# Where the weight tiles and the split x tiles begin in SBUF: 64 more bytes in two tiles

## The chip, the cores and the metric

The kernel runs on one core of a Trainium2 chip. The metric is the device time of one execution in microseconds (us), as the median of several executions. A profile is a record of one execution.

## What is computed

One decoder block on a sequence of 2048 tokens with 1024 channels, batch 1. The input is normalised (RMSNorm), scaled and shifted by a conditioning vector, and projected by one wide matrix. From that projection two branches are fed, a gated causal convolution and an RWKV-7 recurrence; each is projected again, the two are mixed by sigmoid gates, and an output projection is added to the input through a gate.

```python
h = _rmsnorm(x, norm_g[l]) * (1.0 + scale[:, None, :]) + shift[:, None, :]
p = jnp.einsum('bsd,de->bse', h, w_in[l])
c_val, c_gate, c_og, ts, r_og, g_conv, g_rwkv = jnp.split(p, SPLITS, axis=-1)
y_conv = _conv_branch(c_val, c_gate, c_og, conv_k[l], ...)
y_rwkv = _rwkv7_branch(ts, r_og, rwkv_mu[l], ...)
m = jax.nn.sigmoid(g_conv) * y_conv + jax.nn.sigmoid(g_rwkv) * y_rwkv
out = jnp.einsum('bsd,de->bse', m, w_out[l])
x = x + gate[:, None, :] * out
...
return _rmsnorm(x, final_g)
```

## The kernel before

The sequence is worked in four blocks of 512 tokens (`TB`). Channels lie on the 128 partitions, eight tiles of 128 channels (`KT`).

The large projections keep float32 accuracy by splitting each operand into a high part rounded to the matmul's format and the remainder, and by three matmuls: high by high, high by low, low by high. `load_w` (from L176) gives a pair of weight tiles `w_hi` and `w_lo`, each 128 partitions by 4096 bytes; at first use it loads a raw tile `w_st`, rounds it (ScalarE, L189), subtracts (GpSimd or VectorE, L191) and stores both parts to DRAM; later uses load the two parts (L182, L183). All three are buffers of one tag in the pool `whl`, seven in a ring. `hsplit` (from L358) makes `h_hi` and `h_lo`, the split x tiles, eight of each, 2048 bytes a partition, in the pool `hp`.

`mm3k` (L199 to L206) is the inner loop. The weight tile is the stationary operand and is loaded into the array for each matmul; the split x tile streams past it. In the first phase (`msplit` 2) a block's 512 columns are streamed in two matmuls of 256; this is the group `ps_main<-h_hi,w_hi` and its two sisters at L206. In the second phase (`msplit` 1) the two branch projections stream 512 columns (`o_hi`, `u_hi`, `m_hi` against `w_hi` and `w_lo`, L206 too), and the output projection (L1090 to L1092) has the operands the other way round: the mixed tiles `m_hi`, `m_lo` or `o_hi`, `o_lo` stationary, the weight tiles streaming 256 columns.

Between the projections the order on TensorE is that of the tile scheduler. In each group of two channel tiles (`pair`, called from `group`) the recurrence adds small matmuls (L534, L597, L657, L666, L684, L689, L695, L708) and a chain of GpSimd steps (L625, L627); the convolution (`conv`) is 31 VectorE steps per channel tile (L774).

SBUF is given out in two stacks, every tile rounded up to 32 bytes a partition. The left one begins with 1152 bytes of scratch and constants, then the pool `cst` (identity, the vectors, small columns, `hlg` and `hlb`), then `whl`, then `c1`, `l3`, `lt`. The right one grows down from the top: `e1` (the pair's tiles), `xp`, `hp`, `e2`. `cst` holds 1856 bytes, which is 14.5 times 128, so that `whl` begins at byte 3008. In `e1` the tile `E1` has 2080 bytes, 16.25 times 128. Where tiles begin, as bytes past a multiple of 128:

| tiles | before | after |
|---|---|---|
| `w_hi`, `w_lo`, `w_st` (3008 + 4096 n before) | 64 | 0 |
| `h_hi`, `h_lo` (159680 + 2048 n before) | 64 | 0 |
| the `xp` ring (`xt`, `hf`, `z` ...), `lw`, `la`, `wl`, `M`, `ta` | 64 | 0 |
| `th` and `t1` (one tag in `e2`), `yj` | 0 | 64 |
| `KR`, `As`, `uv`, `tk`, `BK`, `S`, `XO`, `La`, `TT` | 96 | 32 |
| `E2`, `k`, `sq`, `r`, `rh` (after `E1` in `e1`) | 96 | 96 |
| `o_hi`, `o_lo`, `mr`, `xt0` to `xt7` (second phase, right) | 32 | 32 |
| `m_hi`, `m_lo`, `u_hi`, `u_lo` (second phase, left) | 32 | 96 |
| `w_f`, the weight tiles of two of the first projections | 96 | 32 |

Of the kernel before, what the change touches and what calls it, by code (L numbers as in the profile page):

```python
# [9 lines left out]
F32 = mybir.dt.float32  # L10
# [8 lines left out]
P = 128  # L19
D = 1024  # L20
KT = D // P
TB = 512
NTT = TB // P
CH = 64
NCH = TB // CH
# [56 lines left out]
def hybrid_block(ctx: ExitStack, tc: tile.TileContext, x, vecs, convk, w2a2, final_g, ada, w_in, w_co, w_ro, w_o, crow, out,  # L82
# [6 lines left out]
    cst = ctx.enter_context(tc.tile_pool(name="cst", bufs=1))  # L89
# [22 lines left out]
    def vc(name, j=None):  # L112
        o, w = VOFF[name]
        return v[:, o:o + w] if j is None else v[:, o + j:o + j + 1]
# [140 lines left out]
    e1 = early.enter_context(tc.tile_pool(name="e1", bufs=1, side="right"))  # L255
# [9 lines left out]
    nc.sync.dma_start(v, vecs)  # L265
    ab = vc("ada_b")
    hlg = cst.tile([P, KT], F32, name="hlg")
    hlb = cst.tile([P, KT], F32, name="hlb")
    nc.vector.tensor_scalar(out=hlg, in0=vc("conv_ln_g"), scalar1=0.5, scalar2=None, op0=ALU.mult)
    nc.vector.tensor_scalar(out=hlb, in0=vc("conv_ln_b"), scalar1=0.5, scalar2=None, op0=ALU.mult)  # L270

# [167 lines left out]
    def ch3(ap):  # L439
        return ap.rearrange("p (c t) -> p c t", t=CH)  # L440
# [15 lines left out]
    def pair(b, q_, pr, h, lora, uv, Asb, rn, res):  # L456
# [18 lines left out]
        for half in range(2):  # L475
            cs = slice(half * TB // 2, (half + 1) * TB // 2)
            nc.vector.tensor_tensor_scan(out=M[:, cs], data0=keepm, data1=M[:, cs], initial=0.0, op0=ALU.mult, op1=ALU.add)
        E1 = e1.tile([P, NCH, CH + 1], F32, name="E1", tag="E1", bufs=1)
        nc.gpsimd.memset(E1[:, :, 0:1], 1.0)
        nc.scalar.activation(E1[:, :, 1:], ch3(M), AF.Exp, scale=-DECAY)  # L480
        E2 = e1.tile([P, TB], F32, name="E2", tag="E2")
        nc.scalar.activation(E2, M, AF.Exp, scale=DECAY)
        pe = l3.tile([P, NCH], F32, name="pe", tag="pe", bufs=4)
        nc.gpsimd.tensor_copy(pe, E1[:, :, CH])

# [6 lines left out]
        k4 = k.rearrange("p (c e t) -> p c e t", e=2, t=CH)  # L492
        E1x = E1[:, :, 0:CH].rearrange("p (c e) t -> p c e t", e=2)
        E1i = E1[:, :, 1:].rearrange("p (c e) t -> p c e t", e=2)
        E24 = E2.rearrange("p (c e t) -> p c e t", e=2, t=CH)
# [77 lines left out]
    def group(b, g, h, lora, fill):  # L573
        uv = l3.tile([P, NCH, 2, P], F32, name="uv", tag="uv", bufs=2)
        As = [l3.tile([P, 2, NCH, P], F32, name="As", tag="As", bufs=ASB) for _ in range(2)]
        R = [{}, {}]
        rn = lt.tile([P, 2, NCH // 2, 2], F32, name="rn", tag="rn")
        pairs = [pair(b, q, 2 * g + q, h, lora, uv, As[q], rn, R[q]) for q in range(2)]
        for i, q in enumerate(ORD):
            next(pairs[q])  # L580
# [589 lines left out]
```

## Time and profile before

| what | value |
|---|---|
| median of 3 runs | 3031.91 us (3030.95 to 3034.19) |
| the profiled execution's own time | 3047.45 us |
| its span, first to last instruction | 3045.7 us |
| mean granted TensorE clock | 0.975 |
| busy share of the span | TensorE 96%, weight loads 90%, VectorE 68%, GpSimd 41%, ScalarE 31% |
| DMA traffic | 699.24 MB in 368673 packets, mean 230 GB/s |

PE is TensorE's matmuls, PEld its weight loads, DVE VectorE, ACT ScalarE, POOL GpSimd, SP the queue that issues the DMAs. Matmuls overlap in the records, so that the busy time of one is longer than the distance to the next; where it says so, the text takes the distance between the starts in the timeline. In a group's row the numbers are the count, the busy time, the mean duration of one, and the engine's idle time just before them with what ended it.

### The profile page before, as it was taken

The page shows a single profiled execution, that of the slowest core. Times are in us where ns is not written, and L with a number is a line of the kernel's source. Part 1 is how long each engine was busy: PE and PEld are TensorE (multiplying, and loading weights), DVE is VectorE, ACT ScalarE, POOL GpSimd, SP SyncE. Part 2 cuts the span into 40 slices and gives each one's busy share as a digit, 9 for nine tenths or more (in the row PEclk, how much of TensorE's full clock was granted, in tenths as well). Part 3 has the DMA queues.
Part 4 walks back from the last instruction along what each step waited for, and adds up shares of the span by engine and source line. Part 5 has one row for each costly group of instructions (what it writes and reads, how often), then busy time and mean ns, then how long its engine had stood idle before and what let it go on. Part 6 is the DMA issues. An engine that isn't in the chain of part 4 may idle for free.

```text
span 3045.7 us, 64763 instructions
## 1 busy us (share of the span) xinstructions
PE 2914.9 (96%) x25672; PEld 2735.9 (90%) x25672; DVE 2058.4 (68%) x3896; ACT 935.2 (31%) x1759; POOL 1250.1 (41%) x1786
## 2 busy tenths in 40 slices
PE   6999998999999999899999999999999999899998
PEld 6889998989989899899999999999999988788988
DVE  6587877686867676668676767676779635776433
ACT  4433434332323232233232323232323222333201
POOL 3455555434343425143434263625467204565000
PEclk9899999999999999999999999999999999999999
DMA  8666758564758578847474777655647778889674
GB/s 303 205 234 209 251 196 282 199 235 145 250 185 260 187 242 287 235 137 246 151 246 139 246 254 252 199 185 165 212 141 246 229 264 309 320 311 344 239 280 163
DMA packets 368673, 699.24 MB, mean 230 GB/s; under 512 B 136241, under 2 KB 154993, under 8 KB 368370
## 3 DMA queue, kind: packets, MB, share of 16 engines
q1 hardware_dynamic: 368370, 695.10, 68.0%
q8 instruction: 202, 3.31, 0.4%
q14 instruction: 101, 0.83, 0.1%
HBM read 506.14 MB, written 187.70 MB: 228 GB/s over the span
## 4 chain that ended last, share of the span: by engine, by line
PE 61%; DMA 16%; DVE 9%; POOL 7%; SPq 3%; issue 2%; ACT 2%; ACTq 0%; DVEq 0%; POOLq 0%
PE ps_main L206 43%; DMA w_st<-w_in_t 3%; PE aux L534 2%; POOL TT L627 2%; POOL itmp L625 2%; DMA w_st<-w_ro_t 2%; DMA w_st<-w_co_t 2%; PE pout L1091 2%; PE pout L1092 2%; PE pout L1090 2%; PE xo L689 2%; DVE acc L774 1%; DMA w_gr<-grow_d 1%; PE xo L684 1%; PE xo L695 1%
## 5 line engine op out<-in xcount | busy, mean ns | idle before, releaser
L206 PE MATMUL ps_main<-h_hi,w_hi 128*128 128x256 f32 x4608 | 971.3, 289 | 12.2 <-ACT w_hi L189 3.4
L206 PE MATMUL ps_main<-h_hi,w_lo 128*128 128x256 f32 x4608 | 965.4, 289 | 8.5 <-POOL w_lo L191 5.0
L206 PE MATMUL ps_main<-h_lo,w_hi 128*128 128x256 f32 x4608 | 971.3, 289 | 0.0
L206 PEld LDWEIGHTS ps_main<-h_hi,w_hi 128*128 128x128 f32 x4608 | 735.3, 194 | 24.1 <-ACT w_hi L189 3.9
L206 PEld LDWEIGHTS ps_main<-h_hi,w_lo 128*128 128x128 f32 x4608 | 731.8, 194 | 17.5 <-POOL w_lo L191 6.3
L206 PEld LDWEIGHTS ps_main<-h_lo,w_hi 128*128 128x128 f32 x4608 | 733.9, 194 | 8.1 <-issue 0.5
L774 DVE SCALAR_TENSOR_TENSOR acc<-u,ck,acc 128x512 f32<-128x512 f32 x928 | 698.6, 753 | 20.8
L625 POOL TENSOR_TENSOR itmp<-La,TT 128x126 f32<-128x126 f32 (+22 forms) x496 | 180.2, 363 | 140.9 <-DMA La<-dA 106.1
L627 POOL TENSOR_TENSOR TT<-TT,itmp 128x126 f32<-128x126 f32 (+22 forms) x496 | 188.2, 379 | 37.3
L681 ACT ACTIVATE Se<-S,pe 128x128 f32<-128x128 f32 x256 | 89.0, 395 | 239.4 <-DVE S L699 239.2
L191 POOL TENSOR_TENSOR w_lo<-w_st,w_hi 128x1024 fp32r<-128x1024 f32 x47 | 113.6, 2417 | 112.8 <-ACT w_hi L189 106.2
L699 DVE TENSOR_TENSOR S<-xo,Se 64x128 f32<-64x128 f32 x256 | 73.5, 287 | 104.1 <-PE xo L695 100.8
L189 ACT CAST w_hi<-w_st 128x1024 fp32r<-128x1024 f32 x71 | 74.2, 1046 | 182.4 <-DMA w_st<-w_in_t 147.4
L534 PE MATMUL aux<-KR,BK 64*128 64x128 f32 x1024 | 121.5, 307 | 7.4 <-POOL BK L517 4.1
L534 PEld LDWEIGHTS aux<-KR,BK 64*128 64x128 f32 x1024 | 104.2, 208 | 18.7 <-POOL BK L517 4.3
L562 POOL TENSOR_TENSOR BK<-BK,pe 128x1024 f32<-128x1024 f32 x32 | 62.0, 1939 | 140.7 <-PE aux L534 113.1
L691 DVE TENSOR_TENSOR uv<-xo,rn 64x256 f32<-64x256 f32 x128 | 53.8, 420 | 90.7 <-PE xo L689 88.8
L686 DVE TENSOR_TENSOR XO<-xo,XO 128x256 f32<-128x256 f32 x128 | 53.7, 420 | 89.9 <-PE xo L684 70.5
L537 DVE TENSOR_TENSOR As<-aux,maskA 128x512 f32<-128x512 f32 x128 | 83.8, 685 | 36.9 <-PE aux L534 35.6
L684 PE MATMUL xo<-S,KR 128*128 128x128 f32 x512 | 83.0, 285 | 15.0 <-DVE S L699 14.9
L786 ACT ACTIVATE th<-ps_main 128x512 f32<-128x512 f32 x64 | 38.1, 596 | 190.1 <-PE ps_main L206 168.9
L431 ACT ACTIVATE t<-ps_main,mu 128x512 f32<-128x512 f32 x96 | 65.6, 683 | 97.4 <-PE ps_main L206 90.4
(301 smaller groups left out, 5318.2 us busy)
## 6 DMA issues: line engine op xcount, KB each, us to landing
w_hi<-kh_in SPq DMA_DIRECT2D x219, 512.0 KB, 5.1
w_lo<-kl_in SPq DMA_DIRECT2D x219, 512.0 KB, 4.0
w_st<-w_in_t SPq DMA_DIRECT2D x73, 512.0 KB, 4.9
kh_in<-w_hi SPq DMA_DIRECT2D x71, 512.0 KB, 2.9
kl_in<-w_lo SPq DMA_DIRECT2D x71, 512.0 KB, 3.7
w_hi<-kh_ro SPq DMA_DIRECT2D x32, 512.0 KB, 5.6
w_lo<-kl_ro SPq DMA_DIRECT2D x32, 512.0 KB, 5.5
w_hi<-kh_co SPq DMA_DIRECT2D x32, 512.0 KB, 5.5
```

The lines of the kernel that those rows point to most:

```text
L189: nc.scalar.copy(hi, st)
L191: lo_eng.tensor_tensor(out=lo, in0=st, in1=hi.bitcast(F32), op=ALU.subtract)
L206: nc.tensor.matmul(ps[:, qs], ww[:, k, :], aa[k][:, qs], start=(k == 0 and t == 0 and q == 0), stop=(k == KT - 1 and t == 2 and q == ms - ...
L431: nc.scalar.activation(t1, ps, AF.Identity, scale=mu1[:, mi:mi + 1])
L534: nc.tensor.matmul(pA[hh][:, c // 2, es], BK[hs, cc, es], KR[hs, cc, es], start=(c == 0), stop=(c == 3), skip_group_check=True)
L537: nc.vector.tensor_tensor(out=Asb[:, hh, c4 * 4:c4 * 4 + 4, :].rearrange("p (a e) n -> p a (e n)", e=2), in0=pA[hh], in1=flat(maskA).unsqu ...
L625: nc.gpsimd.tensor_tensor(out=tmp[:, :ni, :nt], in0=La[:, j:j + 1, j + 1:].broadcast_to([P, ni, nt]), in1=TT[:, :ni, j:j + 1].broadcast_to ...
L627: nc.gpsimd.tensor_tensor(out=TT[:, :ni, j + 1:], in0=TT[:, :ni, j + 1:], in1=tmp[:, :ni, :nt], op=ALU.add)
L681: nc.scalar.mul(Se[:, q, :], Sg[:, q, :], R[q]["pe"][:, c:c + 1])
L684: nc.tensor.matmul(xo[:, q, :], R[q]["KR"][:, cc, es], Sg[:, q, :], start=(q == 0), stop=(q == 1), skip_group_check=True)
L699: nc.vector.tensor_tensor(out=Sg[hs, :, hs], in0=xo[hs, 2:4, hs], in1=Se[hs, :, hs], op=ALU.add)
L774: nc.vector.scalar_tensor_tensor(out=acc if i + 1 < HALO else yj, in0=u[:, i:i + TB], scalar=ck[:, j, i:i + 1], in1=acc, op0=ALU.mult, op1 ...
```

## The change

Two tiles get 64 more bytes a partition. `hlb` is taken as the first eight columns of a tile of 24, which moves everything above it on the left stack up by 64 bytes. `E1` gets 67 instead of 65 columns for each of its eight chunks, all at the end; it is taken flat and its first 520 columns are viewed as before, which moves `E1` and everything below it on the right stack down by 64 bytes. No instruction, no shape and no order in the program text is changed.

```diff
-    hlb = cst.tile([P, KT], F32, name="hlb")
+    hlb = cst.tile([P, 24], F32, name="hlb")[:, :KT]
...
-        E1 = e1.tile([P, NCH, CH + 1], F32, name="E1", tag="E1", bufs=1)
+        E1 = e1.tile([P, NCH * (CH + 3)], F32, name="E1", tag="E1", bufs=1)
+        E1 = E1[:, :NCH * (CH + 1)].rearrange("p (c t) -> p c t", c=NCH)
         nc.gpsimd.memset(E1[:, :, 0:1], 1.0)
         nc.scalar.activation(E1[:, :, 1:], ch3(M), AF.Exp, scale=-DECAY)
```

## Prediction, made before the changed kernel ran

> **What bounds the kernel now.** I read the page first: its shares, the chain, the costliest groups.
>
> ```profile
> span 3045.7 us, 64763 instructions
> PE 2914.9 (96%) x25672; PEld 2735.9 (90%) x25672; DVE 2058.4 (68%) x3896; ACT 935.2 (31%) x1759; POOL 1250.1 (41%) x1786
> ...
> PE ps_main L206 43%; DMA w_st<-w_in_t 3%; PE aux L534 2%; POOL TT L627 2%; POOL itmp L625 2%; DMA w_st<-w_ro_t 2%; DMA w_st<-w_co_t 2%; PE pout L1091 2%; PE pout L1092 2%; PE pout L1090 2%; PE xo L689 2%; DVE acc L774 1%; DMA w_gr<-grow_d 1%; PE xo L684 1%; PE xo L695 1%
> ...
> L206 PE MATMUL ps_main<-h_hi,w_hi 128*128 128x256 f32 x4608 | 971.3, 289 | 12.2 <-ACT w_hi L189 3.4
> L206 PE MATMUL ps_main<-h_hi,w_lo 128*128 128x256 f32 x4608 | 965.4, 289 | 8.5 <-POOL w_lo L191 5.0
> L206 PE MATMUL ps_main<-h_lo,w_hi 128*128 128x256 f32 x4608 | 971.3, 289 | 0.0
> ```
>
> TensorE works almost all the time, and 43% of the chain is one line, the matmuls of the split x tiles with the weight tiles: 3 x 4608 = 13824 of 256 columns. Both their operands are the tiles that the change moves. The view of busy time by stretch puts TensorE at 2313 of 2392 us in the first phase (then weight loads, VectorE, ScalarE, GpSimd, the granted clock, the DMA share and GB/s); the view of its waits shows how little it loses to transfers.
>
> ```profile
> 60.00:2452.00 2392.00, 2313.22 (x22197) 2215.94 (x22195) 1707.98 (x3139) 761.50 (x1400) 1064.97 (x1646) 0.97 0.66 215
> ```
> ```profile
> PE ps_main L206 <- DMA w_lo<-kl_in: 3.5, 3, 2.5
> ...
> PE pout L1091 <- DMA w_lo<-kl_o: 2.0, 1, 2.0
> ```
>
> So the question is the distance between matmul starts, and whether it depends on where the tiles begin. The timeline of TensorE gives it, in undisturbed stretches at the full clock: first phase, front stage (weights `w_f`), output projection with `o` tiles and with `m` tiles, branch projection of 512 columns.
>
> ```profile
> 1501.46 0.40 PE L206 MATMUL ps_main<-h_hi,w_lo 128*128 128x256 f32 x2
> ...
> 1504.34 0.40 PE L206 MATMUL ps_main<-h_hi,w_lo 128*128 128x256 f32 x2
> ```
> ```profile
> 56.25 0.64 PE L206 MATMUL ps_f<-h_hi,w_f 128*128 128x256 f32 x4
> ...
> 57.45 0.40 PE L206 MATMUL ps_f<-h_lo,w_f 128*128 128x256 f32 x2
> ```
> ```profile
> 2855.35 0.28 PE L1090 MATMUL pout<-w_hi,o_hi 128*128 128x256 f32 x1
> ...
> 2857.80 0.28 PE L1090 MATMUL pout<-w_hi,o_hi 128*128 128x256 f32 x1
> ```
> ```profile
> 2718.86 0.28 PE L1090 MATMUL pout<-w_hi,m_hi 128*128 128x256 f32 x1
> ...
> 2721.35 0.28 PE L1090 MATMUL pout<-w_hi,m_hi 128*128 128x256 f32 x1
> ```
> ```profile
> 2841.00 0.39 PE L206 MATMUL ps_main<-u_hi,w_hi 128*128 128x512 f32 x1
> ...
> 2845.90 0.39 PE L206 MATMUL ps_main<-u_hi,w_hi 128*128 128x512 f32 x1
> ```
>
> First phase: 12 rows of two, 24 matmuls in 2.88 us, 120.0 ns each. Front: 10 in 1.20 us, 120 ns. Output projection with `o`: 21 in 2.45 us, 116.7 ns; with `m`: 21 in 2.49 us, 118.6 ns. 512 columns: 21 in 4.90 us, 233.3 ns, which is 116.7 for each 256.
>
> **What these distances say of alignment.** By the table of addresses: in the first phase weight and x tile both begin 64 past a multiple of 128, and the distance is 120. In the front the weight begins 96 past, x 64 past: 120 again. In the output projection the streaming weight begins 64 past, the stationary tile 32 past: 116.7 with `o`, 118.6 with `m`. At 512 columns the streaming tile is 32 past: no more per column than the best. So streaming from 64 past a multiple of 128 does not by itself cost 120, and the weight's move from 64 to 96 changed nothing. On the other side `o` and `m` differ by 1.9 ns with the same shapes and the same remainder, so something besides shape, perhaps the addresses' relation, is worth up to 3.3 ns. None of these has both operands on a multiple of 128: that case no row shows.
>
> **The change part by part.** No instruction is added or removed, and no wait; `E1` keeps its two disjoint writes, so I expect the same order on every engine. Four effects are left.
>
> *First-phase matmuls.* Bounds from the rows: from 116.7, the best distance for 256 columns, to 123.3, as far above 120 as that is below (no row is there; it is the observed spread turned over). That is 13824 x 3.3 ns = 46 us either way on TensorE. What of it reaches the end: all of it if TensorE stays the bound (97% busy in the phase), or the share of these matmuls that lies on the chain. The chain has 43% of 3045.7, 1310 us; all matmuls of L206 take 13824 x 0.120 + 1344 x 0.233 = 1972 us (1344 are those of 512 columns); 1310/1972 is 0.66, so 31 us. I take 0, because the two rows with equal structure and different weight alignment (first phase and front) agree at 120.
>
> *Second phase.* The `o` tiles stay, the weights move by 64; 1536 matmuls of the output projection, half with `o`: if these went from 116.7 to 120, 768 x 3.3 ns = 2.5 us more; if the `m` half went from 118.6 to 116.7, 768 x 1.9 ns = 1.5 us less. I take 0.
>
> *VectorE and ScalarE.* The convolution's steps read `u` at starts 4 bytes apart, so every remainder is already in this row; and ScalarE writes from PSUM into `th` (0 past) and `rk` (96 past):
>
> ```profile
> L774 DVE SCALAR_TENSOR_TENSOR acc<-u,ck,acc x928: 704/756/1139, 151.0 to 2407.6; 128x512 f32<-128x512 f32 x186
> ```
> ```profile
> L754 ACT ACTIVATE th<-ps_main 128x512 f32<-128x512 f32 x64 | 38.0, 594 | 160.4 <-PE ps_main L206 108.3 <-issue 43.2 <-DMA gr_d<-th 3.7
> ...
> L557 ACT COPY rk<-aux 128x512 f32<-128x512 f32 x32 | 18.8, 586 | 1.5 <-PE aux L287 0.8
> ```
>
> Minimum and median are 7% apart over all starts, and 586 to 594 ns over remainders 0 and 96: no cost to move, none to gain. `th` loses its alignment at no more than 8 ns. The cover is TensorE: VectorE is at 71% of the first phase.
>
> *DMA.* Stores from `th` and `yj` (0 past), `oc` and `vv` (96 past), and the weight traffic (64 past), to landing:
>
> ```profile
> ro_d<-th SPq DMA_DIRECT2D x32, 256.0 KB, 4.2
> bv_d<-vv SPq DMA_DIRECT2D x32, 256.0 KB, 2.3
> ...
> y_d<-yj SPq DMA_DIRECT2D x32, 256.0 KB, 3.6
> o_d<-oc SPq DMA_DIRECT2D x32, 256.0 KB, 4.6
> ```
> ```profile
> w_hi<-kh_in SPq DMA_DIRECT2D x219, 512.0 KB, 5.1
> ```
>
> The aligned stores (4.2 and 3.6) are not quicker than the others (2.3 and 4.6). If weight loads nevertheless became quicker, the two longest waits of TensorE for them come to 3.5 + 2.0 = 5.5 us, about the most it could give directly; slower by a tenth, 0.5 us each, they would still land within the ring of seven tiles. I take 0 from a range of -6 to +3.
>
> A rule that speaks for a gain here: the Trainium skill, "DMA: Bandwidth & Descriptors", section "How a descriptor splits into AXI transactions", says that transactions start on 256-byte boundaries, so that a run beginning off one needs one more. By it a 4096-byte row of a weight tile, now 192 past such a boundary and then on it, goes from 17 transactions to 16; by my estimate from the page that is up to 6% of these transfers, and the sum would still be within the 6 us above. The landing rows do not show such an order.
>
> **Sum.** 0 + 0 + 0 + 0. The profiled execution, 3047.45 us by itself (span 3045.7 and 1.75 around it), is 15.5 us over the median of the runs, 3031.91; with no term to subtract I give the median, a little rounded down for the DMA term: 3031 us. A measurement of this kernel can tell about 0.2%, 6 us, from no change.
>
> **The rivals.** *Same pace, same time* (my forecast): 3026 to 3038.
>
> *Alignment frees the matmuls.* The 120 would be a collision between the weight load and the streaming read, and the new addresses would end it, as `o` shows at 116.7. For it: `o` against `m`, equal but for the place. Against it: the front's 120. Price 31 us by the chain's share and 46 in full: 3001 to 2986; a half step to 118.6 gives 1.4/3.3 of 31, 13 us, 3019.
>
> *Alignment frees them altogether.* Then only the weight loads would set the distance. Matmuls of 128 columns with a load each show that floor:
>
> ```profile
> 1500.66 0.60 PE L695 MATMUL xo<-uv,tk 128*128 128x128 f32 x4
> 1500.99 0.28 PE L695 MATMUL xo<-uv,tk 128*128 128x128 f32 x1
> ```
>
> Three distances from the first start to the last matmul's start take 0.33 us, 110 ns. From 120 to 110 is 13824 x 10 ns = 138 us, 91 by the chain's share: 2941, down to 2894. Against it: the 512-column stretch, with its streaming tile at another remainder (32), does not beat 116.7 per 256 either. The Trainium skill, "TensorE: Matmul & The Clock Gate", section "Back-to-back issue gap", has 262 cycles for 256 columns, by my estimate 109 ns at its 2.4 GHz; it does not speak of alignment, and no full-clock stretch quoted here reaches it.
>
> *Slower: the same collision gets worse.* Place: L206 in the first phase. The distance between the two operands' starts changes by 128 bytes, as the weights go up by 64 and x goes down by 64. If the new relation costs what the good one saves, 123.3 ns, the kernel ends at 3031.9 + 31 to 46: 3062 to 3078. It decides from 120.7 ns on, where 13824 x 0.7 x 0.66 passes 6 us. For it: nothing but that relation has been seen to matter; against it: 120 is the longest steady distance in any stretch read here.
>
> **How the numbers follow.** Same pace 0.46. Freed to 116.7 or half of it 0.33. Freed altogether 0.04. Worse 0.11. A drift of some 10 us with unchanged distances, from throttling that falls otherwise (the clock's mean is 0.97 in the first phase), 0.06, half to each side for lack of a sign. Faster 0.33 + 0.04 + 0.03 = 0.40; within 0.2% 0.46; slower 0.14. The range takes in the freed case to its full price, 2986, and the drift and the small end of the worse one, to 3050; left out are the 0.04 below and most of the 0.11 above. The likeliest case alone has 3026 to 3038.
>
> **What would show it.** Right: the row of `ps_main<-h_hi,w_hi` keeps a mean of 289 ns, and 24 matmuls in an undisturbed stretch take 2.88 us; the landing times of weight tiles and the 756 of L774 stay. The freed case shows 2.80 us for 24 and less TensorE time with more waits on VectorE and GpSimd. The worse case shows over 2.90 us. The prediction fails if the distance depends on the relation of the two starts, which the rows here can't separate from the order of the matmuls.

## The result, and the profile after

The changed kernel takes 3023.47 us (median of 11 executions, 3016.2 to 3037.63), the kernel before 3034.06 us (median of 11): a ratio of 0.9965, 95% interval 0.9952 to 0.9979, or 10.6 us less. The profiled execution took 3030.42 us. From its page (span, busy times, the chain by engine, groups, a DMA row):

```profile
span 3028.7 us, 64763 instructions
PE 2896.6 (96%) x25672; PEld 2719.3 (90%) x25672; DVE 2058.4 (68%) x3896; ACT 935.8 (31%) x1759; POOL 1252.0 (41%) x1786
...
PE 56%; DMA 16%; DVE 10%; POOL 9%; issue 3%; SPq 3%; ACT 3%; ACTq 0%; DVEq 0%; POOLq 0%
...
L206 PE MATMUL ps_main<-h_hi,w_hi 128*128 128x256 f32 x4608 | 966.6, 288 | 12.2 <-DVE carry L437 3.6
...
L775 DVE SCALAR_TENSOR_TENSOR acc<-u,ck,acc 128x512 f32<-128x512 f32 x928 | 698.0, 752 | 20.8
...
w_hi<-kh_in SPq DMA_DIRECT2D x219, 512.0 KB, 5.2
```

Before, the chain by engine was this:

```profile
PE 61%; DMA 16%; DVE 9%; POOL 7%; SPq 3%; issue 2%; ACT 2%; ACTq 0%; DVEq 0%; POOLq 0%
```

The counts of instructions are those of before, and on each engine their order is too; line numbers from L477 on are one higher. VectorE's busy time is the same 2058.4, the convolution step 752 against 753 ns, a weight load lands after 5.2 against 5.1 us. What went down is TensorE's busy time, by 18.3 us. The mean of an L206 matmul fell by 1 ns only, but busy times overlap, and the distance between starts says more. TensorE's timeline of the changed kernel, first phase:

```profile
1501.06 0.40 PE L206 MATMUL ps_main<-h_hi,w_lo 128*128 128x256 f32 x2
...
1502.96 0.40 PE L206 MATMUL ps_main<-h_lo,w_hi 128*128 128x256 f32 x2
```

Eight rows of two lie between the two starts: 16 matmuls in 1.90 us, 118.75 ns, where it was 120.0. Over all undisturbed first-phase stretches (full granted clock, no wait in front of the matmul) the mean is 118.72 (119.74 before). The output projection with `o` tiles went the other way:

```profile
2855.08 0.28 PE L1091 MATMUL pout<-w_hi,o_hi 128*128 128x256 f32 x1
...
2857.60 0.28 PE L1091 MATMUL pout<-w_hi,o_hi 128*128 128x256 f32 x1
```

21 matmuls in 2.52 us, 120.0 ns; it was 116.7.

### The profile page after: what moved, and what is told of

Same layout as the page of the kernel before. It is cut to its first block, busy times and chain, and to the rows that moved or that the text cites. A ratio compares the mean times of both kernels' runs of the same rounds, so it can differ in the third digit from the quotient of the medians.

```text
span 3028.7 us, 64763 instructions
## 1 busy us (share of the span) xinstructions
PE 2896.6 (96%) x25672; PEld 2719.3 (90%) x25672; DVE 2058.4 (68%) x3896; ACT 935.8 (31%) x1759; POOL 1252.0 (41%) x1786
## 4 chain that ended last, share of the span: by engine, by line
PE 56%; DMA 16%; DVE 10%; POOL 9%; issue 3%; SPq 3%; ACT 3%; ACTq 0%; DVEq 0%; POOLq 0%
PE ps_main L206 41%; POOL TT L628 3%; POOL itmp L626 3%; DMA w_st<-w_in_t 2%; DMA w_st<-w_ro_t 2%; PE aux L535 2%; DMA w_st<-w_co_t 2%; PE pout L1092 2%; PE pout L1093 2%; PE pout L1091 2%; DMA w_gr<-grow_d 1%; PE xo L690 1%; DVE acc L775 1%; PE xo L696 1%; PE xo L685 1%
## 5 line engine op out<-in xcount | busy, mean ns | idle before, releaser
L206 PE MATMUL ps_main<-h_hi,w_hi 128*128 128x256 f32 x4608 | 966.6, 288 | 12.2 <-DVE carry L437 3.6
L206 PE MATMUL ps_main<-h_lo,w_hi 128*128 128x256 f32 x4608 | 967.1, 288 | 0.0
L206 PE MATMUL ps_main<-h_hi,w_lo 128*128 128x256 f32 x4608 | 960.7, 288 | 5.9 <-DMA w_lo<-kl_in 3.3
L206 PEld LDWEIGHTS ps_main<-h_hi,w_hi 128*128 128x128 f32 x4608 | 726.7, 191 | 24.1 <-DVE carry L437 3.9
L206 PEld LDWEIGHTS ps_main<-h_hi,w_lo 128*128 128x128 f32 x4608 | 723.4, 191 | 13.9 <-DMA w_lo<-kl_in 3.7
L206 PEld LDWEIGHTS ps_main<-h_lo,w_hi 128*128 128x128 f32 x4608 | 725.7, 191 | 8.1 <-issue 0.2
L191 POOL TENSOR_TENSOR w_lo<-w_st,w_hi 128x1024 fp32r<-128x1024 f32 x47 | 113.3, 2411 | 107.9 <-ACT w_hi L189 91.9
L535 PE MATMUL aux<-KR,BK 64*128 64x128 f32 x1024 | 114.9, 294 | 3.8 <-POOL TT L621 2.2
L535 PEld LDWEIGHTS aux<-KR,BK 64*128 64x128 f32 x1024 | 98.1, 196 | 14.5 <-POOL TT L621 2.4
L690 PE MATMUL xo<-XO,As 64*64 64x64 f32 x1024 | 90.6, 227 | 4.8 <-DVE XO L687 4.7
```

The lines of the kernel that those rows point to most:

```text
L191: lo_eng.tensor_tensor(out=lo, in0=st, in1=hi.bitcast(F32), op=ALU.subtract)
L206: nc.tensor.matmul(ps[:, qs], ww[:, k, :], aa[k][:, qs], start=(k == 0 and t == 0 and q == 0), stop=(k == KT - 1 and t == 2 and q == ms - ...
L535: nc.tensor.matmul(pA[hh][:, c // 2, es], BK[hs, cc, es], KR[hs, cc, es], start=(c == 0), stop=(c == 3), skip_group_check=True)
L690: nc.tensor.matmul(xo[pr_, q, hs], As[q][pr_, hh, c, kcol(e)], XO[pr_, c, q, hs], start=(q == 0 and hh == 0), stop=(q == 1 and hh == 1), s ...
```

## The experiments

Three theories went in. *Multiples of 128*: a tile that begins on a multiple of 128 bytes is read faster. *Order*: the distance hangs on the order of the three matmuls and on which half of the PSUM bank (the memory that takes the results) is written. *Relation*: what counts is d, the start of the streaming tile minus the start of the stationary one, modulo some power of two; the expected texts of the two halves take the same difference the other way round, so that their 64 is d = 192 here. In bytes modulo 256, weight and x tiles begin at 192 and 192 before (d = 0), and at 0 and 128 after (d = 128).

### Half of the change: the weight tiles alone

```diff
-    hlb = cst.tile([P, KT], F32, name="hlb")
+    hlb = cst.tile([P, 24], F32, name="hlb")[:, :KT]
```

> Only hlb's tile grows: weight tiles begin on a multiple of 128 (0 past a multiple of 512), split x tiles stay 64 past (448 past a multiple of 512). Relation theory (the distance of 256-column matmuls follows the difference of the two starts): the difference goes from 0 to 64, neither the 0 of before (120.0 ns) nor the 128 of after (118.7 ns); the first phase's distance differs from 120.0 and the time follows it by about 9 us per ns. Own-alignment theory (each operand by itself): the weight on a multiple of 128 gives its part alone, between 118.7 and 120.0 ns, 0 to 11 us faster. Rival, that the gain is not in the matmuls' distance: 120.0 ns and yet another time than before.

3013.51 us against 3036.65 of before, measured beside it: 0.9929 (0.9907 to 0.9950). One half of the change gains more than twice what the whole does. Now d is 192 - 0 = 192. Its timeline:

```profile
1819.90 0.39 PE L206 MATMUL ps_main<-h_lo,w_hi 128*128 128x256 f32 x2
...
1822.62 0.39 PE L206 MATMUL ps_main<-h_lo,w_hi 128*128 128x256 f32 x2
```

Twelve rows of two, 24 matmuls in 2.72 us: 113.3 ns, below anything seen before the change.

### The other half: the x tiles alone

```diff
-        E1 = e1.tile([P, NCH, CH + 1], F32, name="E1", tag="E1", bufs=1)
+        E1 = e1.tile([P, NCH * (CH + 3)], F32, name="E1", tag="E1", bufs=1)
+        E1 = E1[:, :NCH * (CH + 1)].rearrange("p (c t) -> p c t", c=NCH)
```

> Only E1 grows: split x tiles begin on a multiple of 128 (384 past a multiple of 512), weight tiles stay 64 past (448). Relation theory: the difference is 64 as with the weights alone, so the same first-phase distance and the same time as that kernel, to 0.2%. Own-alignment theory: the rest of the gain, so that the two kernels' gains add up to the 10.6 us of the whole change. In the output projection nothing moves but the relation stays: 116.7 ns with o tiles, about 118 with m tiles.

3019.27 us, 0.9941 (0.9919 to 0.9962). Two stretches of its timeline:

```profile
1819.79 0.39 PE L206 MATMUL ps_main<-h_lo,w_hi 128*128 128x256 f32 x2
...
1822.51 0.39 PE L206 MATMUL ps_main<-h_lo,w_hi 128*128 128x256 f32 x2
```
```profile
2069.98 0.40 PE L206 MATMUL ps_main<-h_hi,w_hi 128*128 128x256 f32 x2
...
2072.81 0.40 PE L206 MATMUL ps_main<-h_hi,w_hi 128*128 128x256 f32 x2
```

The first has 113.3 ns again (24 in 2.72 us), the second 117.9 (24 in 2.83). Both paces occur with the same d, each held through a stretch; the mean over all is 114.8. The two halves have different tiles on a multiple of 128 but the same d, 192, and the same pace, and their times are 5.8 us apart, within the 0.2% expected. Their gains, 23.1 and 17.4 us, don't add up to that of the whole. That speaks for the relation.

### The whole change once more

> The changed kernel once more beside its two halves: ratio 0.995 to 0.998 to before, first-phase distance 118.7 ns by every theory.

3029.06 us, 0.9980 (0.9965 to 0.9995), undisturbed mean 118.71 ns. On the same chip, against the same 3036.65 us of before, the whole gains 7.6 us, the weights alone 23.1 and x alone 17.4.

### A map of starts

All other work is left out here, and the one execution ran at the full granted clock. 16 stationary tiles and 16 streaming tiles begin at 0, 32, ... 480 modulo 512, `wa` to `wp` and `xa` to `xp`; each pair runs 48 matmuls into one half of a PSUM bank (L34), and once more into both halves in turn (L42).

```python
for w in ws:
    for t in xs:
        for i in range(48):
            nc.tensor.matmul(ps[:, 0:N], w, t[:, 0:N], start=(i == 0), stop=(i == 47))
```

> Matmuls alone: 16 weight tiles wa to wp that begin 0, 32 ... 480 bytes past a multiple of 512 against 16 streaming tiles xa to xp that do the same, 48 matmuls of 256 columns for each pair, first into one half of a bank (L39), then in turn into both halves as mm3k does (L47). All other work of the block is left out; the output is a copy of the input. Relation theory: the distance is constant along the diagonals of the table, 120.0 where the starts are equal, and both ways of writing give one table. Own-alignment theory: rows and columns with 0, 128, 256, 384 stand out. Order theory (the way the two halves of a bank are written sets 120 against 116.7): the first table is 116.7 throughout, the second 120. Carried over from the traces: w 448, x 448 gives 120.0; w 160, x 448 gives 116.7; w 0, x 384 gives 118.7; w 160, x 0 gives 120.0.

Rows of the timeline, 48 matmuls each (start, then the time of the 48). The stationary tile `wc` begins at 64, `wd` at 96:

```profile
228.67 6.02 PE L34 MATMUL pa<-xc,wc 128*128 128x256 f32 x48 [0.52 <-ACT sink L35]
235.21 5.87 PE L34 MATMUL pa<-xd,wc 128*128 128x256 f32 x48 [0.52 <-ACT sink L35]
241.59 5.92 PE L34 MATMUL pa<-xe,wc 128*128 128x256 f32 x48 [0.52 <-ACT sink L35]
248.03 6.02 PE L34 MATMUL pa<-xf,wc 128*128 128x256 f32 x48 [0.52 <-ACT sink L35]
254.56 5.96 PE L34 MATMUL pa<-xg,wc 128*128 128x256 f32 x48 [0.52 <-ACT sink L35]
261.04 5.97 PE L34 MATMUL pa<-xh,wc 128*128 128x256 f32 x48 [0.52 <-ACT sink L35]
267.52 5.72 PE L34 MATMUL pa<-xi,wc 128*128 128x256 f32 x48 [0.52 <-ACT sink L35]
273.76 5.95 PE L34 MATMUL pa<-xj,wc 128*128 128x256 f32 x48 [0.52 <-ACT sink L35]
280.23 6.02 PE L34 MATMUL pa<-xk,wc 128*128 128x256 f32 x48 [0.52 <-ACT sink L35]
...
338.22 6.02 PE L34 MATMUL pa<-xd,wd 128*128 128x256 f32 x48 [0.52 <-ACT sink L35]
...
377.07 5.73 PE L34 MATMUL pa<-xj,wd 128*128 128x256 f32 x48 [0.52 <-ACT sink L35]
```

From `xc` to `xj` d goes from 0 to 224 in steps of 32; at `xk`, d = 256, the time of d = 0 is back. `xd,wd` (d = 0) and `xj,wd` (d = 192), 32 bytes further up, repeat `xc,wc` and `xi,wc`. The row's time is 47 distances and the last matmul. The distance between starts, the first seven of each row left out, as the median over the 64 pairs with the same d, beside the places of the kernels that have this d:

| d | distance, ns | where |
|---|---|---|
| 0 | 120.0 (1 of 64 pairs, the first of the run, 155.8) | first phase before (120.0) |
| 32 | 116.7 (1 of 64 pairs 117.8) | `o` before (116.7) |
| 64 | 117.8 (5 of 64 pairs 113.3) | `o` in the unaligned kernel below (117.8) |
| 96 | 120.0 | `o` after (120.0); front `w_f` before (120) |
| 128 | 118.7 (6 of 64 pairs 120.0) | first phase after (118.7) |
| 160 | 118.7 (9 of 64 pairs 117.3) | `m` before (118.6) and after (118.7) |
| 192 | 113.3 (2 of 64 pairs 117.8) | first phase of both halves (113.3, some stretches 117.8) |
| 224 | 118.3 | |

Every place of 256 columns that the prediction read fits. Of the 512 pairs 488 lie within 0.5 ns of their median, for both ways of writing PSUM alike; the other 24 are those in brackets, so that something besides d sets the pace of some pairs. *Multiples of 128* fails (`wa` with `xa`, `xe`, `xi` and `xm`, for instance, has both tiles on one; d is 0 or 128 there, and the pace nothing special), and so does *order*.

### The control: both tiles on multiples of 256, d as before

```diff
+    hlb = cst.tile([P, 24], F32, name="hlb")[:, :KT]
...
+        E1 = e1.tile([P, NCH * (CH + 1) + 48], F32, name="E1", tag="E1", bufs=1)
```

> `hlb` has 24 columns as in the changed kernel and `E1` has 48 more columns, so that weight tiles and split x tiles both begin on multiples of 256 bytes (and so of 128), while the x tile's start minus the weight tile's is 0 modulo 256, as it is before. If multiples of 128 are what counts: first-phase distance 118.7 ns or less and the time of the changed kernel again, 0.9965 of before or lower; DMA with its starts on 256 bytes can only help. If the relation of the two starts counts: 120.0 ns, and 1.000 of before within 0.002; the output projection with `o` goes from 116.7 to 120.0 ns (difference 96), 2.5 us more.

3031.82 against 3035.70 us: 0.9991 (0.9975 to 1.0007), no change that can be told. The timeline and a DMA row of its page:

```profile
1820.41 0.40 PE L206 MATMUL ps_main<-h_lo,w_hi 128*128 128x256 f32 x2
...
1822.81 0.40 PE L206 MATMUL ps_main<-h_hi,w_lo 128*128 128x256 f32 x2
```
```profile
w_hi<-kh_in SPq DMA_DIRECT2D x219, 512.0 KB, 5.1
```

20 matmuls in 2.40 us, 120.0 ns. The output projection with `o`, now at d = 96, went to 120.0 as expected. Alignment as such gains nothing, neither on TensorE nor in the landing of the weight tiles.

### The counterpart: neither tile on a multiple of 64, d = 192

```diff
+    hlb = cst.tile([P, 16], F32, name="hlb")[:, :KT]
...
+        E1 = e1.tile([P, NCH * (CH + 1) + 8], F32, name="E1", tag="E1", bufs=1)
```

> `hlb` has 16 columns and `E1` has 8 more, so that weight tiles begin 96 and split x tiles 32 past a multiple of 128: neither on one, and the x tile's start minus the weight tile's is 192 modulo 256. Relation: first-phase distance 113.3 ns in most stretches, some at 117.8, mean near 115, and 0.993 to 0.994 of before, as the two halves of the change have. Multiples of 128: no gain, 120 ns and 1.000 of before.

3011.93 us: 0.9911 (0.9887 to 0.9935). 32 bytes more in each of two tiles gain more than the 64 of the change. Timeline and page:

```profile
1819.97 0.39 PE L206 MATMUL ps_main<-h_hi,w_lo 128*128 128x256 f32 x2
...
1822.69 0.39 PE L206 MATMUL ps_main<-h_hi,w_lo 128*128 128x256 f32 x2
```
```profile
PE 2852.5 (95%) x25672; PEld 2671.4 (89%) x25672; DVE 2055.8 (68%) x3896; ACT 934.6 (31%) x1759; POOL 1249.5 (41%) x1786
...
PE 47%; DMA 19%; POOL 12%; DVE 12%; issue 4%; SPq 3%; ACT 3%; POOLq 0%; ACTq 0%; DVEq 0%
```

24 in 2.72 us, 113.3 ns. The two kernels with the aligned and the unaligned pair settle it: the relation decides, alignment does not.

### The second phase moved too

The x half, run again for comparison, and two unused tiles that move the stationary tiles of the output projection:

```diff
+    oa.tile([P, 40], F32, name="opad", tag="opad")
...
+    hl.tile([P, 56], F32, name="mpad", tag="mpad")
```

> The half that moves x alone once more, for the comparison with the other three on one chip: 0.994 of before within 0.002 by the relation; first phase near 114.8 ns, output projection 116.7 with `o` and 118.4 with `m`.

> The half of the change that moves x alone, and two unused tiles that move `o_hi`, `o_lo` down by 160 bytes and `m_hi`, `m_lo` up by 224, so that the difference of streaming and stationary start is 192 modulo 256 in the output projection too. Relation: output projection 113.3 ns with `o` (116.7 with x alone) and with `m` (118.4), 768 x 3.3 + 768 x 5.1 = 6.5 us less on TensorE in the second phase, where little waits: 4 to 6.5 us below x alone in the same call, near 0.992 of before. If the output projection's distances have another cause: 116.7 and 118.4 stay and the time is that of x alone.

The x half: 3015.44 us, 0.9920 (0.9897 to 0.9943). With the second phase: 3007.75 us, 0.9906 (0.9885 to 0.9928), the lowest median of all; 7.7 us below the x half, though that difference of two medians has no interval of its own. Its timeline, first the output projection with `o`, then the projections of 512 columns, then the output projection with `m`:

```profile
2819.77 0.28 PE L1093 MATMUL pout<-w_hi,o_hi 128*128 128x256 f32 x1
...
2822.26 0.28 PE L1093 MATMUL pout<-w_hi,o_hi 128*128 128x256 f32 x1
```
```profile
2860.18 0.39 PE L206 MATMUL ps_main<-m_lo,w_hi 128*128 128x512 f32 x1
...
2864.99 0.39 PE L206 MATMUL ps_main<-m_lo,w_hi 128*128 128x512 f32 x1
```
```profile
2689.72 0.28 PE L1094 MATMUL pout<-w_lo,m_hi 128*128 128x256 f32 x1
...
2691.96 0.28 PE L1095 MATMUL pout<-w_hi,m_lo 128*128 128x256 f32 x1
```

`o`: 22 matmuls in 2.49 us (one of the rows between holds two), 113.3 ns. 512 columns: 21 in 4.81 us, 229.0, where 233.3 stood. Here the moved tile streams and the weight is stationary, so that d is 0 - 192, which is 64; that this helps was not expected, and over 1344 matmuls it is 1344 x 4.3 ns = 5.8 us. This `m` stretch: 19 in 2.24 us, 117.9, the second pace again, while others with `m` run at 113.4. Over all undisturbed stretches the means are 114.6 with `o` and 115.1 with `m`, not the 113.3 expected throughout.

### Where the rest of the gain stays

At d = 192 TensorE should save some 13824 x 4.9 ns = 68 us, and only 17 to 24 us arrive. For the control and the unaligned kernel with d = 192 I summed the time from each matmul's start to the next one's over the whole trace, by what follows it:

| TensorE time, us | d = 0 | d = 192 | difference |
|---|---|---|---|
| L206, full clock, next matmul without a wait | 2077.7 | 2005.4 | -72.3 |
| L206, then an idle of over 60 ns | 79.8 | 106.9 | +27.1 |
| all matmuls in spells of a lower granted clock | 105.8 | 131.4 | +25.6 |
| other matmuls, then an idle of over 60 ns | 38.3 | 45.0 | +6.7 |
| the others | 697.4 | 692.2 | -5.2 |
| sum | 2999.0 | 2980.9 | -18.1 |

So in this pair of profiles some 34 us go into waits (25 to 49 in the other three profiles of kernels with d = 192 in the first phase alone, against the same control). Matmuls that fall into a spell of a lower clock are missing from the first row, so that the +25.6 is not all loss. Which waits grow is in the view of TensorE's waits (total, times, longest), before and then the unaligned kernel:

```profile
PE xo L684 <- DVE S L699: 14.9, 12, 2.4
...
PE late L739 <- POOL XO L734: 3.4, 2, 1.8
```
```profile
PE xo L685 <- DVE S L700: 21.6, 16, 3.8
...
PE late L740 <- POOL XO L735: 9.8, 8, 2.4
```

They are the recurrence's own steps; by engine, the rows of the whole view sum to 85.5 us for VectorE and 17.2 for GpSimd before (84.6 and 15.9 in the control), 105.3 and 24.8 here.

One pair of profiles says little of the spells of a lower clock, as their length differs between profiles of one kernel (163.9 and 149.0 us in the two of the x half; with d = 0, 156.8 before and 126.8 in the control). All the executions on record say more. The mean granted clock, the share of its full speed that TensorE's clock was given, is 0.9775 over 51 executions of the kernel before and 0.9788 over the 12 of the control, but 0.9741 over 24 executions with d = 192 (the weights alone, x alone twice, the unaligned kernel). A straight line through the 51 has 1.9 us more time for each 0.001 of clock less. By this estimate the lower clock takes some 6 us, and at an equal clock the gain would be some 28 us instead of 22. Why the clock is lower at d = 192, no run here shows.

Is it the convolution, 31 VectorE steps a tile, that keeps the recurrence waiting? Two kernels leave out the first 15 steps of its loop, one with d = 0, one with the x half's d = 192:

```diff
-        for i in range(HALO):
+        for i in range(15, HALO):
```

> The kernel before with the first 15 of the 31 steps of the causal convolution left out (480 VectorE instructions of 752 ns, 361 us less on VectorE; its output is not the reference's). The difference of the first phase's two starts stays 0 modulo 256. This is the base for the next run, and is compared with that. Distance 120.0 ns. If TensorE is the bound as the chain says, little is gained over before: 0.99 to 1.00.

> The same shortened convolution, with x moved so that the difference is 192. The full kernel got 16 to 20 us of some 66 us of TensorE's time (13824 x 4.8 ns), and TensorE's waits for VectorE grew from 85 to 106 us. If VectorE's steps in front of the recurrence's matmuls swallow the rest: with 361 us less on VectorE, at least 35 us come through against the run with equal starts, and waits for VectorE grow by less than 10 us. If the rest is lost otherwise (the granted clock, GpSimd, transfers): again 16 to 25 us.

3062.41 and 3043.20 us (1.0096, 1.0078 to 1.0114, and 1.0022, 1.0007 to 1.0037, of the unshortened kernel before): both are slower than with the whole convolution, which I had not expected; the order of the instructions on TensorE, ScalarE and GpSimd is another in the shorter program, and what in that costs 25 us I did not look for. Against each other, with the same order on every engine, d = 192 gains 19.2 us, as much as in the full kernel. Their pages:

```profile
PE 2908.1 (95%) x25672; PEld 2730.3 (89%) x25672; DVE 1731.9 (57%) x3416; ACT 933.9 (31%) x1759; POOL 1253.0 (41%) x1786
```
```profile
PE 2859.6 (94%) x25672; PEld 2678.5 (88%) x25672; DVE 1732.8 (57%) x3416; ACT 932.4 (31%) x1759; POOL 1253.3 (41%) x1786
```

VectorE has 57% instead of 68%, TensorE's busy time falls by 48.5 us, its waits for VectorE grow from 92.5 to 107.2, by 15 and not by less than 10. So less load on VectorE did not let more of the gain through. This speaks against VectorE's load as what holds it back, but the test is not a clean one: the shortened kernel with d = 0 already has TensorE at 48% of its chain, against 61% before, so that other limits may have come in with the new order. What fits is that the recurrence's chain of small steps between TensorE, VectorE and GpSimd has its own length, and that faster projections leave less work to cover it; that is argued from the waits, not shown.

## Why the prediction was right or wrong

The time lies inside the range, and faster was given 0.40. The likeliest case, "same pace, same time", did not happen. What happened is the half step named under "Alignment frees the matmuls": 118.6 ns, 13 us, 3019; measured were 118.7 ns and 3023.47 us, 10.6 less than before, and 7.6 less the second time. Its price was nearly right, its reason (alignment) wrong. That the range held owes something to this rival's place in it: the forecast itself had no gain.

*First-phase matmuls.* This is the term that failed: "I take 0, because the two rows with equal structure and different weight alignment (first phase and front) agree at 120." They agree by chance, as d is 0 in the one and 96 in the other, and the map has 120.0 for both. Two equal values at two addresses were read as no dependence on addresses, while `o` and `m`, 1.9 ns apart with the same remainder modulo 128, had said that there was one. From mean to mean (119.74 to 118.72) the term measured -1.02 ns x 13824 = -14.1 us on TensorE; the chain's share of 0.66 makes 9.3 us of it, close to what came.

*Second phase.* The upper bound was reached: `o` went from 116.7 to 120.0, 768 x 3.3 ns = 2.5 us more. `m` stayed at 118.7, as its d stayed at 160 (the weights and `m` both moved by 64).

*VectorE, ScalarE, DMA.* The three zeros hold: 753 and 752 ns, 935.2 and 935.8 us busy, 5.1 and 5.2 us to landing. The Trainium skill, "DMA: Bandwidth & Descriptors", section "How a descriptor splits into AXI transactions", lets a 4096-byte run that starts on a 256-byte boundary save one transaction of 17. The weight tiles of the changed kernel, of the control and of the kernel with the weights alone moved start on one, and land in 5.2, 5.1 and 5.3 us against 5.1 before: no run here shows the saving.

*The slower rival* had the right mechanism, that the relation of the two starts changes by 128 bytes, and the wrong sign: 118.7 at d = 128, and no d has more than 120.0. The sentence on what would make the prediction fail named this relation; it could have been used. Tabulating d modulo 256 for the four stretches at hand gives 0, 32, 96, 160 with 120.0, 116.7, 120, 118.6, which shows that the relation could carry all differences, and that d = 128 was unseen.

*Freed altogether.* No relation reaches 110 ns; the best is 113.3. The Trainium skill, "TensorE: Matmul & The Clock Gate", section "Back-to-back issue gap", has 262 cycles for 256 columns, stated of the gap of a matmul by itself and not of pairs of weight load and matmul; that is an estimate of 109 ns at its 2.4 GHz. No undisturbed stretch of 256 columns read here reaches it.

*The chain's share as a price.* At d = 128 it was near. At d = 192 it gives 68 x 0.66 = 45 us, and 17 to 24 came. The share is worked out at one pace, and the chain moved with the step: TensorE's share of it is 61% before and 58% in the control, but 47% in the unaligned kernel, while GpSimd's went from 7% and 8% to 12%.

## What to carry to other kernels

Where TensorE streams short matmuls with a weight load each, tabulate the difference of the operands' SBUF starts modulo 256 bytes: a few unused bytes in an earlier tile change the pace by almost 6% (113.3 to 120.0 ns) and this kernel's time by up to 0.9%, without a further instruction, and aligning both tiles is not the thing to aim at. Test the two halves of a layout change alone; here each half gained two to three times what the whole did beside it (23.1 and 17.4 against 7.6 us). Price a saving on the bounding engine by the chain only for small steps: a larger one meets other limits, here, as far as the waits and the clock tell, the recurrence's steps and a lower granted clock.

## What the runs showed of the hardware

- Steady distance of 256-column matmuls, each with its own weight load, over d modulo 256 bytes in steps of 32: 120.0, 116.7, 117.8, 120.0, 118.7, 118.7, 113.3, 118.3 ns. It holds wherever the pair lies modulo 512, but for 24 of 512 pairs, and for both ways of writing PSUM.
- At d = 192 whole stretches of the kernels run at 113.3 or at 117.8 ns. In the map 2 of 64 pairs do the second, and 5 of 64 at d = 64, whose own pace is 117.8, run at 113.3. At d = 128, 6 of 64 run at 120.0 instead of 118.7, and at d = 160, 9 of 64 at 117.3. What sets which was not found.
- At 512 columns the undisturbed means of the runs are 229.0 ns at d = 64, 233.1 to 233.5 at 96, 192 and 224, and 234.3 at 160: the best d is another than at 256 columns.
- The landing of the weight tiles shows no gain from beginning on a multiple of 256 bytes: 5.1 to 5.3 us where they do (the control, the changed kernel, the weights alone), 5.1 to 5.4 where they do not (before, x alone, the unaligned kernel, the second phase moved too).
- The mean granted clock is 0.9775 over 51 executions with d = 0 in the first phase and 0.9741 over 24 with d = 192.
